# Row statistics of an encoder layer: column sums by a matrix of ones in split f32, root and Newton step on the whole tile

## The chip, the cores and the metric

The kernel runs on one core of one Trainium2 chip. The metric is the device time of one execution in microseconds; the time of a kernel is the median of its runs.

## The reference

One layer of a hybrid encoder in float32: 512 positions, 2048 channels.

```
x1  = rms_norm(x, g1);  proj = x1 @ w_in                       (5 x 1024 columns)
y_conv = silu(layer_norm(depthwise_conv31(u_val * sigmoid(u_gate))))
y_na   = neighbourhood attention of 16 heads on an 8 x 64 grid, with position bias
x  = x + concat(rms_norm(y_conv), rms_norm(y_na)) @ w_out
x2 = rms_norm(x, g2);  up = depthwise_conv3(x2 @ w_up)          (2 x 5632 columns)
x  = x + (silu(gate) * val) @ w_down
return rms_norm(x, g3)
rms_norm(x, g)   = x * rsqrt(mean(x*x) + 1e-6) * g
layer_norm(x)    = (x - mu) * rsqrt(var + 1e-6) * g + b
```

## The kernel before

The work lies transposed: channels on the 128 partitions, the 512 positions in the free dimension. A product is made by *split* matmuls: each f32 operand is written as a high part in the type f32r and the rest (`whi`, `wlo` for weights, lines 115 and 116; `xh`, `xl` and so on for data), and three f32r matmuls are added (`mm3`, lines 128, 131, 132). `weights()` keeps the splits of weights three units ahead of TensorE, in four buffers for each part; ScalarE makes the high part, VectorE the rest.

The order of stages: the input projection (`project`, one block of 512 positions by 128 columns after the other: 48 split matmuls each, results in three PSUM buffers of tag `mm`), with the convolution rows (`glu`, `gated`) and the attention of head pairs (`attend`) worked off behind it; the output projection in two halves (`out_half`: first the convolution group `ma`, then the attention group `mb`, 24 split matmuls for each of 16 blocks); the gated MLP with `w_up` (`up`, `hidden`) and `w_down`.

The normalisations are not applied to the operands but to results, as factors that are equal in all partitions: a tile of 128x512 that holds in each row the factor of each position. There are five of them:

- `rstd1` (from `acc1`): first used in `gated` (line 313) on the result of the first gate projection; with it all results of the input projection
- `rln` (from the `acc` of `group_a`): the LayerNorm of the convolution rows, after their mean (line 343)
- `ra`: used by `read_a` (line 532) on the results of the first half of the output projection
- `rna` (kept in `rb`): used by `after` on the results of the second half
- `rstd2`: used in `hidden` (lines 710 and 711) on the results of `up`

Squares are summed over channel tiles by `sum_sq` into an accumulator of 128x512; what remains is a sum over the 128 partitions, a root, and the factor in all partitions. `rsqrt_steps` does it in two steps. First: four f32 matmuls with a block of the accumulator as weights and one column of ones give the sums of 512 positions as 128x4 (line 216); mean and epsilon, `Sqrt`, reciprocal and one Newton step run on 128x4 (lines 219 to 225); four `tensor_scalar` scale the identity matrix into diagonals `dg` (line 229). Second: one f32 matmul of `dg` with ones spreads the factors over all partitions (line 232), and ScalarE copies them out (line 236).

The mean of the LayerNorm is made by one f32 matmul of the accumulator with ones (line 343).

Statistics are worked as generators: `tick` lets the next step of the first waiting generator be issued behind a block of matmuls. Apart from pinned instructions a scheduler of the framework puts the instructions of each engine in an order when the kernel is built; on the chip each engine works its queue in that order. SP issues the loads in its own order too: weights (`raw`, nine buffers, which the convolution rows `y` share) and the bias tables of the attention (`tab`).

`Sqrt`, `Sigmoid`, `Exp` and `Silu` belong to different function tables of ScalarE; a change of table is an instruction of its own in its queue.

Of the kernel before, what the change touches and what calls it, by code (L numbers as in the profile page):

```python
# [10 lines left out]
F32 = mybir.dt.float32  # L11
F32R = mybir.dt.float32r
AF = mybir.ActivationFunctionType
ALU = mybir.AluOpType
AX = mybir.AxisListType

P = 128
D = 2048
S = 512
# [9 lines left out]
EPS = 1e-6  # L29
# [41 lines left out]
def layer(ctx: ExitStack, tc: tile.TileContext, xT, w_in, w_out, w_up, w_down, par, tab, g3, out):  # L71
    nc = tc.nc
    consts = ctx.enter_context(tc.tile_pool(name="consts", bufs=1))
    wpool = ctx.enter_context(tc.tile_pool(name="w", bufs=3))
    tp = ctx.enter_context(tc.tile_pool(name="t", bufs=NT))
    sm = ctx.enter_context(tc.tile_pool(name="sm", bufs=2))
    dram = ctx.enter_context(tc.tile_pool(name="dram", bufs=1, space=bass.MemoryType.DRAM))
    psm = ctx.enter_context(tc.tile_pool(name="psm", bufs=3, space=bass.MemoryType.PSUM))
    psa = ctx.enter_context(tc.tile_pool(name="psa", bufs=1, space=bass.MemoryType.PSUM))
# [9 lines left out]
    def t2(name, dt=F32):  # L89
        return tp.tile([P, S], dt, tag="t2k", name=name)  # L90
# [8 lines left out]
    def pc(name, i):  # L99
        o = POFF[name] + i  # L100
        return prm[:, o:o + 1]

    ones = consts.tile([P, P], F32, name="ones")
    nc.vector.memset(ones, 1.0)
    ident = consts.tile([P, P], F32, name="ident")
    make_identity(nc, ident)

    def raw_unit(src, n):
        raw = t4([P, U * P], "raw")
        return raw, nc.sync.dma_start(raw[:, :n], src)  # L110
# [78 lines left out]
    def split(src, g, name):  # L189

        h, l = t2(name + "h", F32R), t2(name + "l", F32R)
        nc.scalar.activation(h, src, AF.Copy, scale=g)
        nc.vector.scalar_tensor_tensor(l, src, g, h.bitcast(F32), op0=ALU.mult, op1=ALU.subtract)
        return h, l

    def sum_sq(acc, src, first, to=slice(0, S)):
        if first:
            nc.scalar.activation(acc, src, AF.Square)
        else:
            q = t2("sq")[:, to]  # L200
            nc.scalar.activation(q, src, AF.Square)
            nc.vector.tensor_add(acc, acc, q)

    def stat():
        if where:
            return psa.tile([P, S], F32, tag="tr", name="st", bufs=2)
        return psa.tile([P, 2, S], F32, tag="sc", name="st")[:, 0]

    where = []

    def rsqrt_steps(acc, n, name, to=slice(0, S), keep=True):

        m = (to.stop - to.start) // P
        ps = stat()
        for i in range(m):
            nc.tensor.matmul(ps[:, i:i + 1], acc[:, to.start + i * P:to.start + (i + 1) * P], ones[:, 0:1],
                             start=True, stop=True)
        v, r, y = (sm.tile([P, S // P], F32, tag="rs" + c, name="rs" + c)[:, :m] for c in "vry")
        nc.vector.tensor_scalar(v, ps[:, :m], 1.0 / n, EPS, op0=ALU.mult, op1=ALU.add)
        nc.scalar.activation(r, v, AF.Sqrt)  # L220
        nc.vector.reciprocal(r, r)
        nc.vector.tensor_mul(y, v, r)
        nc.vector.tensor_mul(y, y, r)
        nc.vector.tensor_scalar(y, y, -0.5, 1.5, op0=ALU.mult, op1=ALU.add)
        nc.vector.tensor_mul(y, y, r)

        dg = t2("dg")
        for i in range(m):
            nc.vector.tensor_scalar(dg[:, i * P:(i + 1) * P], ident, y[:, i:i + 1], None, op0=ALU.mult)
        yield  # L230
        ps = stat()
        nc.tensor.matmul(ps[:, :m * P], ones, dg[:, :m * P], start=True, stop=True)
        if not keep:
            return ps[:, :m * P]
        res = t2(name)
        nc.scalar.activation(res[:, to], ps[:, :m * P], AF.Copy)
        return res

    def rsqrt_of(*a, **k):
        g = rsqrt_steps(*a, **k)  # L240
        while True:
            try:
                next(g)
            except StopIteration as e:
                return e.value


    xs, x1, early = [], [], []
# [3 lines left out]
    for k in range(KD):  # L252
        x1.append(t2("x"))
        last = pin(nc.sync.dma_start(x1[k], xT[k]))
        h, l = t2("xh", F32R), t2("xl", F32R)
# [3 lines left out]
        if k in (0, 2, 6, 15):  # L259
            raw, i = raw_unit(first[len(early)], U * P)  # L260
# [8 lines left out]
    for step in ORDER:  # L269
        i = next(a_ if step == "a" else q_)  # L270
# [9 lines left out]
    def stats1():  # L280
        for k in range(KD):
            sum_sq(acc1, x1[k], k == 0)
        for _ in range(3):
            yield
        rstd.append((yield from rsqrt_steps(acc1, D, "rstd1")))
# [48 lines left out]
    def group_a():  # L334
        yield
        yield
        acc = t2("acc")
        nc.vector.tensor_add(acc, ys[0], ys[1])
        for i in range(2, NC_):
            nc.vector.tensor_add(acc, acc, ys[i])  # L340
        yield
        ps = psa.tile([P, 2, S], F32, tag="sc", name="st")[:, 0]
        nc.tensor.matmul(ps, ones, acc, start=True, stop=True)
        mu = t2("mu")
        nc.vector.tensor_scalar(mu, ps, 1.0 / CONV, None, op0=ALU.mult)
        acc = t2("acc")
        for i in range(NC_):
            nc.vector.tensor_sub(ys[i], ys[i], mu)
            sum_sq(acc, ys[i], i == 0)
        yield  # L350
        yield
        r = yield from rsqrt_steps(acc, CONV, "rln")
        acc = t2("acc")
        for i in range(NC_):
            nc.vector.tensor_mul(ys[i], ys[i], r)
            nc.scalar.activation(ys[i], ys[i], AF.Silu, scale=pc("lng", i), bias=pc("lnb", i))
            ma.append(split(ys[i], pc("cog", i), "ma"))
        for i in range(NC_):
            sum_sq(acc, ys[i], i == 0)
        for _ in range(RA_AFTER):  # L360
            yield

        ra.append((yield from rsqrt_steps(acc, CONV, "ra")))
# [125 lines left out]
    p, n = -1, 0  # L489
    for step in ORDER:  # L490
        if step == "a":
            if n < 2:
                with tc.issue_after(last.ins):
                    glu(n)
            else:
                glu(n)
            n += 1
            continue
        p += 1
        steps.append(attend(p, *qkv(p)))  # L500
        if p == NORM_AT:
            asteps.append(group_a())
# [259 lines left out]
    def four(first):  # L762

        if first:
            b = psa.tile([P, 2, S], F32, tag="sc", name="pd2")
            return [b[:, 0], b[:, 1]] + [psa.tile([P, S], F32, tag="tr", name="pd", bufs=2) for _ in range(2)]
        return [psm.tile([P, S], F32, tag="mm", name="pd") for _ in range(3)] + [psa.tile([P, S], F32, tag="po",
                                                                                         name="pd")]
# [97 lines left out]
    a = four(True)  # L866
# [19 lines left out]
    a = four(True)  # L886
# [68 lines left out]
```

## Time and profile before

| | us |
|---|---|
| three runs, median (lowest to highest) | 2018.7 (2017.3 to 2019.84) |
| profiled execution | 2021.06 |
| its span | 2019.1 |
| granted TensorE clock, mean | 0.996 |

Times of rows in the profile count from the start of the span. A row of the timeline gives start, duration, engine, line, operation, output and inputs with their shape, and in brackets how long the engine was idle before it and what released it. A row of a group gives the count, the busy time, the mean duration in ns, and the idle time before it. `PE` is TensorE, `PEld` its loading of weights, `ACT` ScalarE, `DVE` VectorE, `SPq` the queue of loads. An f32 matmul counts as two records, an f32r matmul as one.

### The profile page before, as it was taken

How to read it: one execution, taken by the hardware profiler on the slowest of the kernel's cores; microseconds unless marked ns; L12 is line 12 of the kernel's file. 1: busy time of each engine (PE TensorE's matmuls, PEld its weight loads, DVE VectorE, ACT ScalarE, POOL GpSimd, SP SyncE). 2: the span in 40 equal slices, each digit the busy share in tenths (PEclk: the TensorE clock that was granted, in tenths of full speed). 3: DMA queues.
4: the chain of work that ended last, by engine and by line, in shares of the span. 5: the costliest groups of instructions: out<-in, count | busy, mean ns of one | idle time of the engine just before them, and what ended most of it. 6: DMA issues, size and time to landing. Idle time of an engine off the chain costs nothing.

```text
span 2019.1 us, 28450 instructions
## 1 busy us (share of the span) xinstructions
PE 1990.3 (99%) x10511; PEld 1682.7 (83%) x10511; DVE 1608.5 (80%) x2311; ACT 1104.1 (55%) x1724; POOL 230.2 (11%) x318
## 2 busy tenths in 40 slices
PE   8999999998999999999999999999999999999997
PEld 6888888877788888888888888888888888888886
DVE  7985798497556888888888888888888898886764
ACT  6244424446535666666666666666666654554663
POOL 0111111111001111111111111111110400000000
PEclk9999999999999999999999999999999999999999
DMA  7677677676758879899999898998986976665562
GB/s 257 167 222 182 171 176 207 175 191 196 232 140 214 209 204 253 248 247 256 249 255 258 245 267 233 264 242 256 259 236 192 344 261 217 213 217 192 194 212 101
DMA packets 141755, 446.81 MB, mean 221 GB/s; under 512 B 15920, under 2 KB 24112, under 8 KB 140208
## 3 DMA queue, kind: packets, MB, share of 16 engines
q1 hardware_dynamic: 98352, 293.99, 42.6%
q0 software_dynamic: 43264, 151.01, 34.4%
q8 instruction: 82, 1.34, 0.3%
q14 instruction: 57, 0.47, 0.1%
HBM read 426.07 MB, written 111.15 MB: 266 GB/s over the span
## 4 chain that ended last, share of the span: by engine, by line
PE 97%; ACT 1%; DMA 1%; DVE 1%; issue 0%; SPq 0%; POOLq 0%; POOL 0%; DVEq 0%
PE pu L656 25%; PE pu L659 12%; PE pj L128 7%; PE pj L132 7%; PE pd L778 7%; PE pd L779 7%; PE pd L777 7%; PE pj L131 7%; PE po L128 3%; PE po L131 3%; PE po L132 3%; PE pu L128 2%; PE pu L131 2%; PE pu L132 2%; PE po L454 1%; PE sc L414 1%
## 5 line engine op out<-in xcount | busy, mean ns | idle before, releaser
L115 ACT ACTIVATE whi<-raw 128x1024 fp32r<-128x1024 f32 x574 | 607.2, 1059 | 719.2 <-PE pj L131 220.6
L116 DVE TENSOR_TENSOR wlo<-raw,whi 128x1024 fp32r<-128x1024 f32 x574 | 701.1, 1222 | 295.5 <-ACT whi L115 268.2
L656 PE MATMUL pu<-xc,whi 128*128 128x512 f32 x2112 | 748.8, 399 | 0.0
L659 PE MATMUL pu<-xc,wlo 128*128 128x256 f32 x2112 | 593.2, 281 | 0.0
L656 PEld LDWEIGHTS pu<-xc,whi 128*128 128x128 f32 x2112 | 397.0, 188 | 97.0 <-issue 0.2
L659 PEld LDWEIGHTS pu<-xc,wlo 128*128 128x128 f32 x2112 | 399.1, 189 | 0.3 <-issue 0.2
L128 PE MATMUL pj<-xh,whi 128*128 128x512 f32 x640 | 254.4, 399 | 8.0 <-ACT whi L115 8.0
L131 PE MATMUL pj<-xl,whi 128*128 128x512 f32 x640 | 251.4, 393 | 0.0
L132 PE MATMUL pj<-xh,wlo 128*128 128x512 f32 x640 | 251.2, 393 | 0.0
L777 PE MATMUL pd<-whi,ho 128*128 128x512 f32 x616 | 239.5, 389 | 1.6 <-ACT ho L738 1.6
L779 PE MATMUL pd<-whi,ho 128*128 128x512 f32 x616 | 239.6, 389 | 0.6 <-DVE ho L739 0.6
L778 PE MATMUL pd<-wlo,ho 128*128 128x512 f32 x616 | 239.8, 389 | 0.0
L328 DVE SCALAR_TENSOR_TENSOR y<-ch,prm,y 128x507 f32<-128x507 f32 (+14 forms) x240 | 169.8, 739 | 3.3
L128 PEld LDWEIGHTS pj<-xh,whi 128*128 128x128 f32 x640 | 121.3, 189 | 36.3 <-ACT whi L115 9.4
L132 PEld LDWEIGHTS pj<-xh,wlo 128*128 128x128 f32 x640 | 120.9, 189 | 27.9 <-DVE wlo L116 1.5
L131 PEld LDWEIGHTS pj<-xl,whi 128*128 128x128 f32 x640 | 121.2, 189 | 24.7 <-issue 0.7
L184 POOL DMA_DIRECT2D ws<-in_w_down x88 | 79.4, 903 | 545.4 <-DMA ws<-ws 273.6
L777 PEld LDWEIGHTS pd<-whi,ho 128*128 128x128 f32 x616 | 115.7, 188 | 26.3 <-ACT ho L738 1.9
L779 PEld LDWEIGHTS pd<-whi,ho 128*128 128x128 f32 x616 | 115.7, 188 | 25.0 <-DVE ho L739 1.2
L778 PEld LDWEIGHTS pd<-wlo,ho 128*128 128x128 f32 x616 | 115.7, 188 | 24.1 <-DVE wlo L116 0.3
L605 POOL DMA_DIRECT2D raw<-in_w_up x88 | 85.3, 969 | 368.0 <-DMA raw<-in_w_up 142.2
L128 PE MATMUL pu<-xc,whi 128*128 128x256 f32 x352 | 99.7, 283 | 0.5 <-ACT xc L546 0.5
(170 smaller groups left out, 2500.4 us busy)
## 6 DMA issues: line engine op xcount, KB each, us to landing
raw<-in_w_up SPq DMA_DIRECT2D x220, 512.0 KB, 7.3
ws<-in_w_down POOLq DMA_DIRECT2D x132, 512.0 KB, 7.4
raw<-in_w_up POOLq DMA_DIRECT2D x88, 512.0 KB, 9.4
raw<-ws SPq DMA_DIRECT2D x88, 512.0 KB, 3.4
raw<-in_w_in SPq DMA_DIRECT2D x80, 512.0 KB, 5.0
raw<-in_w_down SPq DMA_DIRECT2D x66, 512.0 KB, 3.7
ws<-ws POOLq DMA_DIRECT2D x44, 512.0 KB, 7.2
raw<-in_w_out SPq DMA_DIRECT2D x32, 512.0 KB, 5.2
```

The lines of the kernel that those rows point to most:

```text
L115: i = nc.scalar.activation(hi[:, :n], raw[:, :n], AF.Copy)
L116: j = nc.vector.tensor_sub(lo[:, :n], raw[:, :n], hi[:, :n].bitcast(F32))
L128: i = nc.tensor.matmul(ps, hi[:, a], mh, start=start, stop=False, skip_group_check=more)
L131: nc.tensor.matmul(ps, hi[:, a], ml, start=False, stop=False, skip_group_check=more)
L132: return nc.tensor.matmul(ps, lo[:, a], mh, start=False, stop=stop, skip_group_check=more)
L328: nc.vector.scalar_tensor_tensor(y[:, a:b], h[:, a + j - PAD:b + j - PAD], prm[:, o + j:o + j + 1], y[:, a:b], op0=ALU.mult, op1=ALU.add)
L605: nc.gpsimd.dma_start(a[c], w_up[f, q2], accum_op=ALU.add)
L656: i = nc.tensor.matmul(ps, hi[:, w], m, start=k == 0 and not more, stop=False, skip_group_check=more)
L659: i = nc.tensor.matmul(ps[:, :H], lo[:, w], m[:, :H], start=False, stop=k == U - 1, skip_group_check=more)
L777: nc.tensor.matmul(ps[i], h[:, t], wh[:, d], start=start and not more, stop=False, skip_group_check=more)
L778: nc.tensor.matmul(ps[i], h[:, t], wl[:, d], start=False, stop=False, skip_group_check=more)
L779: return nc.tensor.matmul(ps[i], h[:, tl], wh[:, d], start=False, stop=stop, skip_group_check=more)
```

## The change

The sum over partitions is made in all partitions at once: the accumulator is split into a high part and a rest (`column_sum`), and two f32r matmuls with a matrix of ones as weights add them up into a PSUM tile of 128x512. Mean and epsilon, `Sqrt`, reciprocal and the Newton step then run on the whole tile of 128x512, one half on ScalarE (`Identity`, `Sqrt`, `Square`) and one half on VectorE. The diagonals, the second matmul and the copy are gone. The mean of the LayerNorm is made by `column_sum` too. The chain of one statistic is cut by a `yield` between the sum and the root. Lines of the changed kernel differ from those of the kernel before by +2 ahead of `column_sum` and by -10 or -11 behind `rsqrt_steps`.

```diff
-    ones = consts.tile([P, P], F32, name="ones")
-    nc.vector.memset(ones, 1.0)
+    ones_r = consts.tile([P, P], F32R, name="onesr")
+    nc.vector.memset(ones_r.bitcast(F32), 1.0)
+    eps = consts.tile([P, 1], F32, name="eps")
+    nc.vector.memset(eps, EPS)
...
-    def rsqrt_steps(acc, n, name, to=slice(0, S), keep=True):
-
-        m = (to.stop - to.start) // P
+    def column_sum(acc):
+
+        h, l = t2("ach", F32R), t2("acl", F32R)
+        nc.scalar.activation(h, acc, AF.Copy)
+        nc.vector.tensor_sub(l, acc, h.bitcast(F32))
         ps = stat()
-        for i in range(m):
-            nc.tensor.matmul(ps[:, i:i + 1], acc[:, to.start + i * P:to.start + (i + 1) * P], ones[:, 0:1],
-                             start=True, stop=True)
-        v, r, y = (sm.tile([P, S // P], F32, tag="rs" + c, name="rs" + c)[:, :m] for c in "vry")
-        nc.vector.tensor_scalar(v, ps[:, :m], 1.0 / n, EPS, op0=ALU.mult, op1=ALU.add)
-        nc.scalar.activation(r, v, AF.Sqrt)
+        nc.tensor.matmul(ps, ones_r, h, start=True, stop=False)
+        nc.tensor.matmul(ps, ones_r, l, start=False, stop=True)
+        return ps
+
+    def rsqrt_steps(acc, n, name):
+
+        ps = column_sum(acc)
+        yield
+        nc.scalar.activation(acc, ps, AF.Identity, scale=1.0 / n, bias=eps)
+        r, q = t2(name), t2("rq")
+        nc.scalar.activation(r, acc, AF.Sqrt)
         nc.vector.reciprocal(r, r)
-        nc.vector.tensor_mul(y, v, r)
-        nc.vector.tensor_mul(y, y, r)
-        nc.vector.tensor_scalar(y, y, -0.5, 1.5, op0=ALU.mult, op1=ALU.add)
-        nc.vector.tensor_mul(y, y, r)
-
-        dg = t2("dg")
-        for i in range(m):
-            nc.vector.tensor_scalar(dg[:, i * P:(i + 1) * P], ident, y[:, i:i + 1], None, op0=ALU.mult)
-        yield
-        ps = stat()
-        nc.tensor.matmul(ps[:, :m * P], ones, dg[:, :m * P], start=True, stop=True)
-        if not keep:
-            return ps[:, :m * P]
-        res = t2(name)
-        nc.scalar.activation(res[:, to], ps[:, :m * P], AF.Copy)
-        return res
...
+        nc.scalar.activation(q, r, AF.Square)
+        nc.vector.tensor_mul(q, q, acc)
+        nc.vector.tensor_scalar(q, q, -0.5, 1.5, op0=ALU.mult, op1=ALU.add)
+        nc.vector.tensor_mul(r, r, q)
+        return r
...
         yield
-        ps = psa.tile([P, 2, S], F32, tag="sc", name="st")[:, 0]
-        nc.tensor.matmul(ps, ones, acc, start=True, stop=True)
+        ps = column_sum(acc)
         mu = t2("mu")
```

More of the change, by code (lines that the diff above doesn't have):

```diff
@@ L209, in layer @@
     where = []
-    def rsqrt_steps(acc, n, name, to=slice(0, S), keep=True):
-        m = (to.stop - to.start) // P
+    def column_sum(acc):
+        h, l = t2("ach", F32R), t2("acl", F32R)
+        nc.scalar.activation(h, acc, AF.Copy)
+        nc.vector.tensor_sub(l, acc, h.bitcast(F32))
         ps = stat()
-        for i in range(m):
-            nc.tensor.matmul(ps[:, i:i + 1], acc[:, to.start + i * P:to.start + (i + 1) * P], ones[:, 0:1],
-                             start=True, stop=True)
-        v, r, y = (sm.tile([P, S // P], F32, tag="rs" + c, name="rs" + c)[:, :m] for c in "vry")
-        nc.vector.tensor_scalar(v, ps[:, :m], 1.0 / n, EPS, op0=ALU.mult, op1=ALU.add)
-        nc.scalar.activation(r, v, AF.Sqrt)
-        nc.vector.reciprocal(r, r)
-        nc.vector.tensor_mul(y, v, r)
-        nc.vector.tensor_mul(y, y, r)
-        nc.vector.tensor_scalar(y, y, -0.5, 1.5, op0=ALU.mult, op1=ALU.add)
-        nc.vector.tensor_mul(y, y, r)
-        dg = t2("dg")
-        for i in range(m):
-            nc.vector.tensor_scalar(dg[:, i * P:(i + 1) * P], ident, y[:, i:i + 1], None, op0=ALU.mult)
-        yield
-        ps = stat()
-        nc.tensor.matmul(ps[:, :m * P], ones, dg[:, :m * P], start=True, stop=True)
-        if not keep:
-            return ps[:, :m * P]
-        res = t2(name)
-        nc.scalar.activation(res[:, to], ps[:, :m * P], AF.Copy)
-        return res
[L239 to L245, printed above, removed]
+        nc.tensor.matmul(ps, ones_r, h, start=True, stop=False)
[7 more added lines that the diff above has]
+        nc.scalar.activation(r, acc, AF.Sqrt)
+        nc.vector.reciprocal(r, r)
+        nc.scalar.activation(q, r, AF.Square)
[3 more added lines that the diff above has]
+        return r
     xs, x1, early = [], [], []
```

## The prediction

> **What bounds the kernel now.** I read the page first (shares of the span, then the chain that ended last), then the timeline around each of the six places that the change touches, then the groups of instructions for durations, and the windows for the granted clock.
>
> ```profile
> PE 1990.3 (99%) x10511; PEld 1682.7 (83%) x10511; DVE 1608.5 (80%) x2311; ACT 1104.1 (55%) x1724; POOL 230.2 (11%) x318
> ...
> PE 97%; ACT 1%; DMA 1%; DVE 1%; issue 0%; SPq 0%; POOLq 0%; POOL 0%; DVEq 0%
> ```
>
> TensorE is the bound: 97% of the chain. A microsecond less of matmul is a microsecond less of time, unless TensorE then waits; and every new wait of TensorE is paid in full, since hardly any idle time is left to swallow it. So there are two questions: how much TensorE time the new sums save, and whether the new arithmetic on whole tiles makes TensorE wait.
>
> The first statistic shows both:
>
> ```profile
> 37.02 0.69 DVE L202 TENSOR_TENSOR acc<-acc,sq 128x512 f32<-128x512 f32 x1
> ...
> 37.62 1.22 DVE L116 TENSOR_TENSOR wlo<-raw,whi 128x1024 fp32r<-128x1024 f32 x1
> 37.67 0.39 PE L131 MATMUL pj<-xl,whi 128*128 128x512 f32 x1
> ...
> 39.03 0.39 PE L128 MATMUL pj<-xh,whi 128*128 128x512 f32 x1
> ...
> 41.75 0.40 PE L128 MATMUL pj<-xh,whi 128*128 128x512 f32 x1
> ...
> 43.04 0.60 ACT L236 ACTIVATE rstd<-st 128x512 f32<-128x512 f32 x1 [3.75 <-PE st L232]
> ...
> 43.31 0.40 PE L128 MATMUL pj<-xh,whi 128*128 128x512 f32 x1
> ...
> 43.67 0.69 DVE L313 TENSOR_TENSOR gate<-pj,rstd 128x512 f32<-128x512 f32 x1 [2.40 <-ACT rstd L236]
> ...
> 46.06 0.39 PE L128 MATMUL pj<-xh,whi 128*128 128x512 f32 x1
> ```
>
> From 39.03 to 41.75 lie twelve undisturbed split matmuls: 2.72/12 = 0.227 us each, the price of one f32r matmul of 512 columns. From 37.67 to 39.03 lie two of them (0.45) and the four column sums: these cost 1.36 - 0.45 = 0.91 us. From 41.75 to 43.31 lie three (0.68) and the f32 matmul on the diagonal: 1.56 - 0.68 = 0.88 us. The row at 46.06 begins the fourth projection. It is the first to take a PSUM buffer for a second time (three of tag mm) and so needs the gate product, which ends at 43.67 + 0.69 = 44.36. Spare time there: 1.7 us.
>
> **TensorE time saved.** Five roots lose 0.91 + 0.88 each, and the mean of the LayerNorm loses one f32 matmul like that on the diagonal (0.88): 9.8 us. Added are 6 x 2 = 12 f32r matmuls with the ones as weights, at 0.227: 2.7 us. Net **-7.1 us**.
>
> **The new chain behind each sum.** Prices by shape:
>
> ```profile
> L427 DVE RECIPROCAL su<-su 128x2 f32<-128x2 f32 x32 | 5.1, 162 | 14.5 <-ACT s L426 14.5
> L221 DVE RECIPROCAL rsr<-rsr 128x4 f32<-128x4 f32 x5 | 0.9, 177 | 5.5 <-ACT rsr L220 5.5
> L842 DVE RECIPROCAL rsr<-rsr 128x1 f32<-128x1 f32 x4 | 0.6, 158 | 0.3 <-ACT rsr L841 0.3
> L202 DVE TENSOR_TENSOR acc<-acc,sq 128x512 f32<-128x512 f32 x44 | 30.3, 689 | 6.8 <-ACT sq L201 4.9
> L324 DVE TENSOR_SCALAR y<-ch,prm 128x512 f32<-128x512 f32 x8 | 4.3, 540 | 0.0
> L201 ACT ACTIVATE sq<-x 128x512 f32<-128x512 f32 x30 | 17.5, 624 | 21.1 <-DVE x L565 21.1
> L573 ACT ACTIVATE b<-x,prm 128x512 f32<-128x512 f32 x16 | 10.6, 713 | 0.0
> L314 ACT ACT_TABLE_LOAD x4 | 5.1, 1283 | 0.1
> ```
>
> Ahead of the sum stand a copy (0.62) and a subtraction (0.69). Behind it: the Identity with a pointer bias 0.71 (as the pointer scale of L573), a table load 1.28 where another set was in use, Sqrt 0.62, the reciprocal, Square 0.62, a product 0.69, the tensor_scalar 0.54, a product 0.69. The reciprocal of 128x512 is nowhere in the trace. Its rows for 1, 2 and 4 columns (158, 162, 177 ns) lie on a line of 6.5 ns per element, which gives 0.158 + 511 x 0.0065 = **3.5 us**. The ends: 0.69, if it ran like the elementwise rows, and 0.162 + 510 x 0.0075 = 4.0 from the steepest pair. I take 3.5, since the three rows rise by 6.5 ns for each element, where the addition of 512 columns takes 689/512 = 1.3 ns for each. The Trainium skill (VectorE: DVE Perf Modes, First, the fixed hardware budget) says that the reciprocal is an iterative divide with a repeat count of 8; if that meant eight cycles for each element at 0.96 GHz it would be an estimated 4.4 us, and the sum below about 2 us larger.
>
> From Identity to the last product that is 8.65 us, and 0.3 for seven handovers between engines. The old small steps and their diagonal go, but on VectorE and ScalarE only; whether the chain costs time depends on who waits at its end.
>
> *First root (`rstd1`).* The sum's last addition ends at 37.71, the copy at 38.4; VectorE is in a weight split until 38.84 and subtracts until 39.55. In the changed build's queue of TensorE the first new matmul stands three split matmuls later than the old sums, the second five rows behind it: 38.58 and 39.71, both just in time. ScalarE sees the sum at 40.14. Its queue has the table load behind the Identity, which itself waits for the sum, so the load is not hidden any more. 40.14 + 8.65 + 0.3 = 49.1, and the gate product ends at 49.8. The fourth projection is due 22 rows behind the second new matmul, 39.71 + 22 x 0.227 = 44.7. TensorE waits **5.1 us**. With a reciprocal of 0.69 it would be 2.3, with 4.0 5.6.
>
> *`ra`.* The first half of the output projection holds its results in the same three buffers until `ra` is there:
>
> ```profile
> 530.26 0.39 PE L132 MATMUL po<-mah,wlo 128*128 128x512 f32 x1
> 532.05 0.66 PE L402 MATMUL trv<-ident,vw 128*128 128x128 f32 x4 [1.41 <-ACT pt L445]
> ...
> 534.08 0.47 PE L128 MATMUL po<-mah,whi 128*128 128x512 f32 x1
> ...
> 531.42 1.06 ACT L445 ACTIVATE pt<-trp 128x512 f32<-128x512 f32 x2
> 532.38 0.60 ACT L236 ACTIVATE ra<-st 128x512 f32<-128x512 f32 x1
> ...
> 533.01 0.69 DVE L532 TENSOR_TENSOR oa<-po,ra 128x512 f32<-128x512 f32 x1 [0.23 <-ACT ra L236]
> ```
>
> The third output block ends at 530.26; the fourth (534.08) needs the buffer that the product at 533.01 frees at 533.70. No spare time. ScalarE works in order, and its queue in the changed build reads: sum's Identity, two weight splits (the second waits for the end of the third block), the two `pt` copies, and only then the table load, Sqrt and Square. So the chain starts at 532.48 whatever the sum does: 1.28 + 0.62 + 3.5 + 0.62 + 0.69 + 0.54 + 0.69 + 0.3 = 8.2 later `ra` is there (540.7), and the product ends at 541.4 instead of 533.70. **+7.7 us** (4.9 to 8.2 with the ends of the reciprocal). Queued behind Square on ScalarE are `ao`, its split and the `vt` copies of the last head pair; they fit into the fourth block.
>
> *The clock.* A long wait has a second price (the last three numbers of a window's row are the granted clock, the DMA share and GB/s):
>
> ```profile
> 498.73 0.39 PE L131 MATMUL pj<-xl,whi 128*128 128x512 f32 x1
> 504.26 2.08 PE L414 MATMUL sc<-k,q 64*128 64x256 f32 x8 [5.14 <-DVE s L421]
> ...
> 498.00:504.00 6.00, 1.12 (x5) 0.58 (x4) 2.90 (x4) 0.45 (x2) 0.91 (x1) 0.87 1.03 419
> 504.00:509.00 5.00, 4.74 (x15) 3.32 (x16) 4.19 (x9) 3.33 (x12) 0.00 (x0) 0.50 1.00 272
> 509.00:515.00 6.00, 6.00 (x35) 5.21 (x34) 1.55 (x5) 4.71 (x13) 0.00 (x0) 0.98 0.07 12
> ```
>
> The one long wait of today's kernel (5.1 us) left a granted clock of 0.50 for the 5 us behind it, so 2.5 us were lost on top. The wait of 7.7 us gets the same: **+2.5**. The wait of 5.1 us lies at the edge of what one row can tell; I charge half: **+1.25**. By the Trainium skill (TensorE: Matmul & The Clock Gate, What's actually happening) the gate falls to half after an idle window of about 3.4 us, and the window runs freely; the trace agrees with one case (0.87 over 6 us puts the fall 1.6 us before 504). By that rule both waits are long enough to be hit, the shorter one only if the window lies well.
>
> *`rln` and the wait for the tables.* That long wait itself moves:
>
> ```profile
> 472.07 0.58 ACT L236 ACTIVATE rln<-st 128x512 f32<-128x512 f32 x1
> ...
> 489.01 1.10 SPq L464 DMA_DIRECT2D tab<-in_tab  x2
> ...
> 501.10 0.69 DVE L421 SCALAR_TENSOR_TENSOR s<-sc,tab 128x512 f32<-128x512 f32 x1 [5.96 <-DMA tab<-in_tab]
> ```
>
> The `tab` loads stand in SP's queue behind loads of `w_out`, into buffers that ScalarE's last passes over the convolution rows free. Those passes come about 7.5 us later (the chain of `rln` against the 0.58 copy), and one more such load stands ahead of the tables. Against that, the changed build puts the score matmuls 19 split matmuls later (4.3 us), and the two score additions follow each other without the weight split of 1.22 us between them. Tables issued at 496 with 8 to 12 us to land (12.1 today) let TensorE go on between 1.3 us later and 3 us earlier than now. I take **-1.0**, ends -5 (the wait falls short enough to keep the clock) and +2.
>
> *Mean, `rna` and `rstd2`.* At the mean and at `rstd2` the split of the sum has little cover; 0.4 us of wait each, **+0.8** (0 to 2.6, twice 0.62 + 0.69). `rna` is needed 32 us after it is made today, which covers everything. At `rstd2` no table load is needed, but the chain runs through VectorE while the accumulators are folded:
>
> ```profile
> 725.70 1.22 DVE L116 TENSOR_TENSOR wlo<-raw,whi 128x1024 fp32r<-128x1024 f32 x1 [1.80 <-ACT whi L115]
> ...
> 728.47 1.23 DVE L116 TENSOR_TENSOR wlo<-raw,whi 128x1024 fp32r<-128x1024 f32 x1 [1.22 <-ACT whi L115]
> 729.62 0.41 DVE L670 TENSOR_TENSOR vl<-vl,pu 128x256 f32<-128x256 f32 x1
> ...
> 732.98 1.06 ACT L115 ACTIVATE whi<-raw 128x1024 fp32r<-128x1024 f32 x1 [0.66 <-PE pu L656]
> ```
>
> The fold ends at 730.03; the next block of TensorE needs it at 733.0 (the weight split at 732.98 waits for the end of the product before). VectorE gets 0.69 + 3.5 + 1.92 more and 1.9 less to do ahead of it, 4.2 us, of which its idle 1.80 + 1.22 takes 3.0; TensorE comes 1.3 us earlier. 3.0 - 1.2 - 1.3 leaves 0.5 us of cover, less what the changed order costs: **+0.5** (0 to 1.5).
>
> **The sum.** -7.1 + 5.1 + 1.25 + 7.7 + 2.5 - 1.0 + 0.8 + 0.5 = +9.75. The profiled execution took 2021.06 us (span 2019.1 and 2.0 around it), so 2030.8 for one like it; it lies 2.4 above the median of the three runs, 2018.7, from which I forecast **2028.4 us**.
>
> **Rivals.** *TensorE time alone decides.* Its share of the chain speaks for it, and so would an earlier place of ScalarE's root in the queue: if `ra` were ready before the third output block ends and `rstd1` before 44.7, nothing would wait and the saving would stand: 2018.7 - 7.1 = 2011.6, faster. Against it speak the in-order queue at 532.38 and 1.7 us of spare time for an added 5. 8%. *A short reciprocal* (0.69): waits of 2.3 and 4.9, half a clock price (1.25), tables 3 us earlier: -7.1 + 2.3 + 4.9 + 1.25 - 3.0 + 0.8 = -0.9, 2017.8, no change. The three small reciprocals speak against it. 10%. *All at the dear ends* (reciprocal 4.0, clock price paid twice, tables late): -7.1 + 5.6 + 2.5 + 8.2 + 2.5 + 2.0 + 0.8 + 1.5 = +16.0, 2034.7. 20%. The forecast keeps 62%. That the change does not do what it says is excluded by the build: the new instructions are in the queues.
>
> **Numbers.** About 0.2% (4 us) is what a measurement of this kernel can tell from no change. Forecast and dear case are slower by more: 0.82; the short reciprocal is the same: 0.10; faster 0.08. The range 2019 to 2035 takes in the forecast and nearly all of the dear case, and leaves out the faster one and most of the short reciprocal.
>
> **What would show it.** Right: a row RECIPROCAL 128x512 near 3.5 us, five times; TensorE waiting some 5 us for a gate product near 45 us and some 7 us for `oa` at the fourth output block, with a granted clock of 0.50 behind it; matmuls of the sums at 0.23 us apart. Wrong: a reciprocal below 1 us, no wait of TensorE at the fourth projection, or the root of `ra` done while the third output block still runs.

## The result, and the profile after

| | before | after |
|---|---|---|
| median of runs, us | 2019.66 (6 runs, 2017.3 to 2029.33) | 2035.79 (6 runs, 2033.39 to 2040.69) |
| profiled execution, us | 2021.06 | 2034.95 |
| its span, us | 2019.1 | 2032.7 |
| granted TensorE clock, mean | 0.996 | 0.995 |

The changed kernel is slower: ratio 1.0079, 95% interval 1.0066 to 1.0091, 16.1 us between the medians and 13.6 us between the spans. The direction was forecast; the measured time lies 7.4 us above the forecast 2028.4 and 0.8 above the end of the range.

The page of the changed kernel, busy times and shares of the chain that ended last:

```profile
PE 1987.9 (98%) x10471; PEld 1679.9 (83%) x10471; DVE 1628.4 (80%) x2288; ACT 1112.3 (55%) x1735; POOL 231.0 (11%) x318
...
PE 72%; issue 20%; DVE 3%; ACT 3%; DMA 1%; POOL 0%; SPq 0%; POOLq 0%; ACTq 0%; DVEq 0%
```

TensorE works 2.4 us less than before, and VectorE and ScalarE now stand in the chain with 3% each. The 20% of "issue" are almost wholly two stretches behind 1628 us, where the chain runs along the POOL instructions of the output; TensorE is as busy there as before, and the stage table below shows no loss. The prices of the new operations, from the groups of instructions:

```profile
L230 DVE RECIPROCAL ra<-ra 128x512 f32<-128x512 f32 x1 | 3.4, 3353 | 1.7 <-ACT ra L229 1.7
L227 ACT ACTIVATE acc<-st,eps 128x512 f32<-128x512 f32 x4 | 2.7, 687 | 3.8 <-PE st L220 3.8
L233 DVE TENSOR_SCALAR rq<-rq 128x512 f32<-128x512 f32 x5 | 2.1, 424 | 0.1
```

The first root in the timeline of the changed kernel, and the clock behind it and behind `ra` in its windows:

```profile
41.83 0.69 ACT L227 ACTIVATE acc<-st,eps 128x512 f32<-128x512 f32 x1 [1.81 <-PE st L220]
42.54 1.28 ACT L229 ACT_TABLE_LOAD   x1
...
44.50 3.35 DVE L230 RECIPROCAL rstd<-rstd 128x512 f32<-128x512 f32 x1 [3.41 <-ACT rstd L229]
...
50.46 0.69 DVE L303 TENSOR_TENSOR gate<-pj,rstd 128x512 f32<-128x512 f32 x1
...
51.20 0.50 PE L130 MATMUL pj<-xh,whi 128*128 128x512 f32 x1 [4.64 <-DVE gate L303]
```

```profile
51.00:55.00 4.00, 3.80 (x10) 3.01 (x11) 3.23 (x6) 1.74 (x3) 0.00 (x0) 0.61 0.00 0
545.00:550.00 5.00, 4.93 (x12) 3.87 (x13) 4.56 (x8) 0.11 (x1) 0.00 (x0) 0.50 0.00 0
```

The reciprocal holds VectorE for 3.35 us, the fourth projection starts at 51.20, and a granted clock of 0.61 (0.50 behind `ra`) follows. `ra` in the same timeline:

```profile
535.32 1.07 ACT L434 ACTIVATE pt<-trp 128x512 f32<-128x512 f32 x2
536.41 1.28 ACT L229 ACT_TABLE_LOAD   x1
...
538.36 3.35 DVE L230 RECIPROCAL ra<-ra 128x512 f32<-128x512 f32 x1 [1.69 <-ACT ra L229]
...
544.33 0.69 DVE L521 TENSOR_TENSOR oa<-po,ra 128x512 f32<-128x512 f32 x1
...
545.07 0.80 PE L130 MATMUL po<-mah,whi 128*128 128x512 f32 x1 [6.73 <-DVE oa L521]
```

The root stands behind the two `pt` copies and TensorE waits 6.7 us for its end.

**Where the time goes, stage by stage.** I took the same matmul in TensorE's queue of two traces (for instance the 60th of the input projection with `xl,whi`) and the difference of its start against the profiled execution of the kernel before. What this difference gains within a stage is what the stage costs more. Stages by the time of the kernel before: first root 32 to 125 us, sums of mean and `rln` 125 to 497, tables and `ra` 497 to 541, `rna` 541 to 661, end of the output projection 661 to 710, `rstd2` 710 to 743, rest up to 1997. The rows from e_rstd1 on are the experiments of the next section.

| kernel | first root | mean, rln | tables, ra | rna | end of out | rstd2 | rest |
|---|---|---|---|---|---|---|---|
| forecast | +5.0 | -1.4 | +7.9 | -1.3 | 0 | -0.4 | 0 |
| after | +7.1 | -1.7 | +7.3 | -1.3 | +1.8 | -0.4 | 0.0 |
| e_rstd1 | +7.0 | 0.0 | -1.8 | -0.1 | +4.9 | +0.2 | -0.6 |
| e_ra | +1.0 | 0.0 | +6.4 | 0.0 | +0.7 | +0.3 | -0.6 |
| e_rest | +1.0 | -1.7 | +0.8 | -1.3 | +5.9 | +0.4 | +1.4 |
| e_rest2 | +0.4 | -1.7 | -0.1 | -1.3 | +5.3 | -0.3 | +1.3 |
| e_norecip | +2.0 | -1.7 | +0.2 | -1.3 | 0.0 | -0.4 | +1.4 |
| e_hoist | +6.6 | -1.8 | +7.6 | -1.3 | +0.1 | -0.6 | +1.6 |
| e_ra4 | +7.3 | -1.7 | +10.0 | -1.3 | -0.1 | -0.4 | 0.0 |
| e_ra4cut | +7.3 | -1.7 | +2.1 | -1.3 | +1.2 | -0.7 | 0.0 |
| e_ars | +0.6 | -1.8 | +3.9 | -1.3 | +1.8 | -0.4 | +1.3 |
| e_after_xt | +7.3 | -1.8 | +7.3 | -1.3 | -0.1 | -0.6 | +1.6 |
| e_before_xt | +0.9 | 0.0 | -2.4 | 0.0 | -0.1 | -0.3 | +1.5 |
| e_rest_xt | +1.2 | -1.7 | +1.0 | -1.3 | -0.1 | -0.6 | 0.0 |
| e_rest_ars | -0.1 | -1.7 | -1.9 | -1.3 | -0.1 | -0.9 | 0.0 |
| e_all_ars | +1.0 | -1.8 | -2.5 | -1.3 | -0.1 | -0.9 | +1.6 |

How far one trace can be trusted: at 32 us, before the first root, the traces lie between -1.2 and +1.7 us of the profiled execution of before. In the column of the first root the six other traces with the old root lie between -0.1 and +1.2, and nearly all of it arises from 32 to 36 us: four of them wait there 0.8 to 1.1 us for the split of a weight, as the changed kernel does (0.91 us at 35.33) and the profiled execution of before does not. From 36 to 125 us these six gain at most 0.05. The +1.3 to +1.6 of the last column is a halved clock: near 1590 us all sixteen traces have a wait of TensorE of 1.6 us and one of 0.6 us behind it, and in eight of them the granted clock fell there. The windows of e_norecip, and of before, where it did not fall:

```profile
1586.00:1590.00 4.00, 3.21 (x8) 2.30 (x9) 3.97 (x10) 2.36 (x7) 1.61 (x3) 0.65 1.03 398
```

```profile
1586.00:1590.00 4.00, 1.78 (x7) 1.14 (x7) 2.90 (x6) 3.04 (x8) 1.57 (x3) 1.00 1.03 400
```

### The profile page after: what moved, and what is told of

It reads as the page before. It is cut to its first block, busy times and chain, and to the rows that moved or that the text cites. A ratio compares the mean times of both kernels' runs of the same rounds, so it can differ in the third digit from the quotient of the medians.

```text
span 2032.7 us, 28340 instructions
## 1 busy us (share of the span) xinstructions
PE 1987.9 (98%) x10471; PEld 1679.9 (83%) x10471; DVE 1628.4 (80%) x2288; ACT 1112.3 (55%) x1735; POOL 231.0 (11%) x318
## 4 chain that ended last, share of the span: by engine, by line
PE 72%; issue 20%; DVE 3%; ACT 3%; DMA 1%; POOL 0%; SPq 0%; POOLq 0%; ACTq 0%; DVEq 0%
PE pu L645 24%; PE pu L648 12%; PE pj L130 6%; PE pj L134 6%; PE pj L133 6%; PE po L130 3%; PE po L133 3%; PE po L134 3%; PE pu L134 2%; PE pu L133 2%; PE pu L130 2%; DVE y L318 1%; ACT whi L117 1%; PE po L443 1%; PE sc L403 1%
```

## The experiments

The kernels were timed in four groups, each together with the kernel before; its medians were 2019.71 (23 runs), 2020.5 (17), 2019.63 (23) and 2020.04 (21). The last group (e_rest_ars and e_all_ars) ran on another chip than the other three, so its kernels are set against those of other groups by their ratios.

### One part at a time

Three kernels split the change: the whole tile for `rstd1` alone, for `ra` alone, and for the mean, `rln`, `rna` and `rstd2` together. The edit of the first (the function with the whole tile stands beside the old one):

```diff
-        rstd.append((yield from rsqrt_steps(acc1, D, "rstd1")))
+        rstd.append((yield from rsqrt_whole(acc1, D, "rstd1")))
```

> Against the kernel before, only rstd1 goes by the whole tile. Theory (waits where a result needs a buffer back): the two new matmuls save 0.91 + 0.88 - 2 x 0.227 = 1.3 us; TensorE waits about 4.8 us at the fourth projection for the gate product, the clock is halved behind it for some 3.4 us (1.9 us lost), and VectorE, held by the chain, is late at a weight split near 105 us (0.85 us): about +6 us, 2025 to 2027. Rival (TensorE time alone): -1.3 us. Rival (the larger loss lies in an interplay of the six places): less than half of +6. If the start (first weights) is again 1.7 us later than in the kernel before, the order of the loads or the constants makes it, not the statistic.

Measured 2028.32 us, ratio 1.0047 (1.0035 to 1.006): +8.6, above the 2025 to 2027 expected. Both rivals are refuted: the first root costs 7.0 by the stages, as in the changed kernel. The start is late again (first matmul by 1.3 us, 0.5 from the ninth `xl` matmul on), but e_norecip and e_ra4, with the same first instructions as the changed kernel, are 0.3 us early there: chance. On top come 4.9 us at the end of the output projection, a part of the code that this kernel does not touch, and 1.8 are given back at the tables.

```diff
-        ra.append((yield from rsqrt_steps(acc, CONV, "ra")))
+        ra.append((yield from rsqrt_whole(acc, CONV, "ra")))
```

> Against the kernel before, only ra goes by the whole tile. Theory: -1.3 us of TensorE time, a wait of 7.1 us for oa at the fourth output block and 2.4 us of halved clock behind it: about +8.2 us, 2026 to 2028. Rival (TensorE time alone): -1.3 us.

Measured 2028.76 us, ratio 1.0047 (1.0034 to 1.006): +9.0 where the theory had +8.2. TensorE's waits of this kernel from 495 to 560 us (total, times, longest):

```profile
PE po L131 <- DVE oa L551: 6.9, 1, 6.9
PE sc L433 <- DVE s L440: 3.8, 1, 3.8
```

```diff
+        ps = column_sum(acc)                    # the mean
...
-        r = yield from rsqrt_steps(acc, CONV, "rln")
+        r = yield from rsqrt_whole(acc, CONV, "rln")
...                                              # rna and rstd2 likewise
```

> Against the kernel before, the mean, rln, rna and rstd2 go by the new way, rstd1 and ra by the old one. Theory: 0.4 + 3 x 1.3 = 4.3 us of TensorE time saved, about 1 us more from the stage of the tables, 1 us lost at rstd2: about -4 us, 2014 to 2016, and so faster than both kernels. Rival (the longer chain costs VectorE or the loads elsewhere, the extra wait near 722 us among them): 0 or slower. If the wait of 1.75 us near 722 us is there again, it belongs to this part of the change and not to the shift in time that rstd1 and ra cause.

Measured 2020.53 us, ratio 1.0006 (0.9997 to 1.0014): no gain. The expectation of -4 failed. The three parts add up to 18.4 us, the whole change cost 16.1. In the trace of e_rest the 1.7 and 1.3 us of the sums are there, but +0.8 at the tables and +5.9 at the end of the output projection eat them. That end is the surprise; but this profiled execution took 2027.23 us and was the slowest of twelve, so that a loss of this size is not that of a typical run. There, ScalarE of this kernel waits:

```profile
706.74 0.72 ACT L564 ACTIVATE xc<-t 128x256 fp32r<-128x256 f32 x2 [4.88 <-DMA xt<-xt]
```

A tile `xc` takes a buffer of the common pool out of which `xt` is still being written to memory. The kernel before has no such wait.

> The run with mean, rln, rna and rstd2 alone once more, for its trace: in the first one TensorE stood 4.5 us near 706 us behind writes of xt to memory, with 1.4 us of halved clock. Theory (chance in the DMA's timing): the wait near 706 us is another one, between 0 and 4 us, and the time is 2018 to 2022. Rival (the change shifts that stage for good): again over 4 us and about 2027.

Measured 2024.81 us in its one run, and the wait again, one run of the same kernel later:

```profile
705.48 0.72 ACT L564 ACTIVATE xc<-t 128x256 fp32r<-128x256 f32 x2 [4.79 <-DMA xt<-xt]
```

So the wait is no accident of one execution. Its length varies between kernels (0.3 us in e_norecip, 0.5 in e_ra4, 1.2 in e_ra, 2.35 in the changed kernel, 4.0 in e_rstd1), and, as the median of e_rest suggests, between executions of one kernel; no trace of a run near that median was taken.

### What the buffers of xt cost

```diff
-        r = t2("xt").rearrange("p (t k) -> p t k", t=S // P)
+        r = tp.tile([P, S], F32, tag="xt", name="xt", bufs=3).rearrange("p (t k) -> p t k", t=S // P)
...
-NT = 75
+NT = 72
```

> The run with mean, rln, rna and rstd2 alone, with three buffers of their own for the tiles xt that are written out to memory (72 instead of 75 in the common pool). In all changed kernels a tile xc takes a buffer of the common pool out of which xt is still being written, ScalarE waits up to 4.9 us for that write and TensorE up to 4.5. Theory (the buffer is what costs): that wait is gone, the wait of TensorE near 706 us too, and 4 us come off: 2015 to 2018, below the kernel before. Rival (the writes are late whatever waits for them, and xt itself waits then): no change, 2020 to 2022.

> The changed kernel with three buffers of their own for xt. Theory: its wait of 1.75 us near 720 us goes: 1.5 to 2 us below the changed kernel, 2033.5 to 2034.5. Rival: no change.

> The kernel before with three buffers of their own for xt, as a control. It has no such wait: no change, 2018.5 to 2020.5. If it gains or loses over 2 us, the buffers do something else than to free xc.

Measured 2019.14 us (ratio 0.9995, 0.9986 to 1.0003), 2033.05 (1.0061, 1.0048 to 1.0074) and 2019.27 (0.9995, 0.9986 to 1.0003). In all three the column "end of out" falls to -0.1, and the wait of `xc` is gone. The changed kernel comes down by 2.7 us in the median, and by 1.9 in that stage of the traces; the control does not move. e_rest_xt came down by 1.4 only, less than expected, and stands beside the kernel before instead of 3 us below. So the collision of `xc` and `xt` is shown as one cost of the change, but it is not where the 4 us of TensorE time went.

### The tables and the chain of rln

What remains in e_rest_xt is the stage of the tables. VectorE before, with the sums of squares of the convolution rows and the `q` product:

```profile
487.94 5.46 DVE L202 TENSOR_TENSOR acc<-acc,sq 128x512 f32<-128x512 f32 x7
494.45 0.68 DVE L380 TENSOR_TENSOR q<-pj,rstd 128x512 f32<-128x512 f32 x1
```

The same in the changed kernel, and TensorE behind it:

```profile
507.19 0.69 DVE L204 TENSOR_TENSOR acc<-acc,sq 128x512 f32<-128x512 f32 x1 [0.47 <-DVE acc L204]
508.93 0.68 DVE L369 TENSOR_TENSOR q<-pj,rstd 128x512 f32<-128x512 f32 x1
509.76 0.76 PE L130 MATMUL po<-mah,whi 128*128 128x512 f32 x1 [2.95 <-DVE q L369]
```

`q` frees a PSUM buffer, and it stands behind sums that the chain of `rln` delays. It starts 14.5 us later, where TensorE is only 6.1 us later than before. The experiment shortens that chain:

```diff
-        nc.scalar.activation(r, acc, AF.Sqrt)
-        nc.vector.reciprocal(r, r)
+        nc.scalar.activation(r, acc, AF.Abs_reciprocal_sqrt)
         nc.scalar.activation(q, r, AF.Square)
```

> The run with mean, rln, rna and rstd2 alone and buffers of their own for xt, now with Abs_reciprocal_sqrt in place of Sqrt and the reciprocal in its three roots. Theory (the time saved ahead of the tables is eaten there because the chain of rln, 3.35 us longer by the reciprocal, brings the squares of the convolution rows later, and q, which frees a PSUM buffer, stands behind their sums on VectorE): the wait of 2.9 us for q falls to under 1, some of the halved clock goes, 2.5 to 4 us below the run with the reciprocal: 2015 to 2017, faster than the kernel before by about 0.15%. Rival (the landing of the bias tables sets that stage whatever rln does): within 1 us of 2019.

Measured 2016.1 us, ratio 0.9978 (0.997 to 0.9987): 3.9 us below the kernel before; e_rest_xt stood at 0.9995. TensorE's waits from 20 to 760 us, of e_rest_xt:

```profile
PE po L131 <- DVE q L398: 2.9, 1, 2.9
PE trp L459 <- ACT s L447: 2.2, 1, 2.2
```

and of e_rest_ars:

```profile
PE st L219 <- DVE s L438: 2.3, 1, 2.3
...
PE po L131 <- DVE q L397: 0.2, 1, 0.2
```

The wait for `q` is gone, and the stage goes from +1.0 to -1.9. The theory holds: the reciprocal with its handovers in the chain of `rln` cost 2.9 us at a place 25 us behind it. What is left there is the landing of the second tables (`s`, 2.3 us).

### The reciprocal and the table load

```diff
-        nc.vector.reciprocal(r, r)
+        nc.vector.tensor_scalar(r, r, 1.0, None, op0=ALU.mult)
```

> The changed kernel with the reciprocal of 128x512 replaced by a multiplication by 1 (the reciprocal is left out). Theory: the row of 3.35 us becomes about 0.43; the wait at the fourth projection falls from 4.8 to about 1.9 us and loses its halved clock and the late weight split (2.9 + 1.9 + 0.85), the wait for oa falls from 7.1 to 4.2 with up to 2.4 us of clock: 8 to 10 us below the changed kernel, 2026 to 2028. Rival (the waits are made by the place of the table load and the root in the queue of ScalarE, the reciprocal runs beside other work): less than 3 us below the changed kernel.

Measured 2022.11 us, ratio 1.0009 (1.0001 to 1.0018): 13.7 us below the changed kernel, more than the 8 to 10 expected. By the stages the first root gains 5.1 us, tables and `ra` together 7.1 (the wait for `q` shrinks from 2.95 to 0.73 us too), and 1.8 come from the end of the output projection. The late weight split stays (0.85 us again), against the expectation. TensorE's waits from 495 to 560 us:

```profile
PE po L130 <- DVE oa L521: 3.8, 1, 3.8
...
PE po L130 <- DVE q L369: 0.7, 1, 0.7
```

```diff
+    warm = consts.tile([P, 1], F32, name="warm")
+    nc.scalar.activation(warm, eps, AF.Sqrt)
```

> The changed kernel with one Sqrt of 128x1 at the start, so that the table for the first root is loaded while ScalarE waits for data. Theory: the load of 1.28 us leaves the chain of rstd1; the wait at the fourth projection falls from 4.8 to 3.5 us; if the clock falls only behind a wait of at least 3.4 us that also lies well, some or all of its 1.9 us go too: 1.3 to 3.2 us below the changed kernel, 2032.6 to 2034.5. Rival (the load is hidden anyway): no change.

Measured 2032.53 us, ratio 1.0054 (1.0036 to 1.0072): 3.3 us below the changed kernel. The wait at the fourth projection is 1.3 us shorter, and the clock falls all the same; timeline, then windows:

```profile
48.77 0.50 PE L132 MATMUL pj<-xh,whi 128*128 128x512 f32 x1 [3.35 <-DVE gate L305]
```

```profile
48.00:51.00 3.00, 2.23 (x6) 1.80 (x7) 2.25 (x4) 0.63 (x1) 0.00 (x0) 0.70 0.00 0
51.00:55.00 4.00, 4.00 (x15) 3.20 (x15) 3.89 (x7) 2.53 (x3) 0.00 (x0) 0.80 0.00 0
```

About 1.6 us are lost behind a wait of 3.35 us, as behind the 4.64 of the changed kernel; behind the 1.7 us of e_norecip the windows show 1.00. The column of the first root falls by 0.5 only, because this trace starts earlier (-1.2 against +0.7) and then waits 1.70 us for the split of a weight at 34.22, where the changed kernel waits 0.91. From 36 us on the root costs 4.9 us instead of 6.2: the early load is worth its 1.3 us. The rest of the 3.3 us lies elsewhere, above all at the end of the output projection (+0.1 against +1.8).

### The place of ra in the queues

```diff
-RA_AFTER = 5
+RA_AFTER = 4
```

> The changed kernel with RA_AFTER = 4 instead of 5: the sum for ra is offered one block of matmuls earlier, and in the queue of ScalarE the table load and the Sqrt then stand directly behind the sum's Identity, ahead of the two weight splits and the two pt copies. Theory (the price of ra lies in the place of the root in an in-order queue): Sqrt near 530 instead of 537.7, ra near 536, the wait for oa falls from 7.1 to under 1 us and its halved clock (2.4 us) goes: 8 to 10 us below the changed kernel, 2026 to 2028. Rival (the chain is simply too long, or VectorE held by the reciprocal delays a weight split by as much): less than 4 us below the changed kernel.

Measured 2036.24 us, ratio 1.0075 (1.0057 to 1.0093): no change, so the expectation failed. The wait for `oa` is gone, but another has taken its place. TensorE's waits up to 800 us, and VectorE's timeline:

```profile
PE po L130 <- DVE vw L378: 8.2, 1, 8.2
```

```profile
530.10 3.35 DVE L230 RECIPROCAL ra<-ra 128x512 f32<-128x512 f32 x1 [2.51 <-ACT ra L229]
...
535.04 0.42 DVE L378 TENSOR_TENSOR vw<-pj,rstd 128x256 f32<-128x256 f32 x1
```

The products `vw` also free a PSUM buffer. They now stand behind the reciprocal, for which VectorE waits 2.5 us with `vw` ready behind it; in the changed kernel `vw` ran at 526.45. The next run puts them ahead again:

```diff
+RA_AFTER = 4
...
         nc.scalar.activation(r, acc, AF.Sqrt)
+        if cut:                  # for ra alone
+            yield
         nc.vector.reciprocal(r, r)
```

> The changed kernel with RA_AFTER = 4 and, for ra alone, a yield between Sqrt and reciprocal. In VectorE's queue the four vw products (which free a PSUM buffer) then stand ahead of the reciprocal of ra again, where with RA_AFTER = 4 alone they stood behind it and cost 8.2 us; in ScalarE's queue Sqrt stands ahead of the weight splits, the Square still behind the pt copies. Theory (ra's price is the order of in-order queues): Square near 536.5, ra near 539, a wait for oa of about 2 us and no halved clock, none for vw: 7 to 8 us below the changed kernel, 2027 to 2029. Rival (every place of the chain costs the same, since some queue holds it): within 3 us of the changed kernel.

Measured 2029.2 us, ratio 1.0046 (1.0033 to 1.006): 6.6 us below the changed kernel, just short of the 7 to 8 expected. Of 6.7 us of wait 1.3 are left:

```profile
PE po L130 <- DVE oa L523: 1.3, 1, 1.3
```

The clock stays up behind it. By the starts of TensorE's matmuls from 529 to 541 us, the same operations on the same data cost 9.5 us at `ra` (6.7 of wait, most of the rest halved clock) or 1.7, by their place in two in-order queues. The whole stage gains only 5.2, since ahead of `ra` e_ra4cut loses 2.6 more than the changed kernel: it waits 2.07 instead of 1.66 us for `s`, and its clock falls behind that (0.57 from 521 to 525 us).

### Everything without the waits

```diff
+    nc.scalar.activation(warm, eps, AF.Abs_reciprocal_sqrt)     # at the start
...
-RA_AFTER = 5
+RA_AFTER = 4
...
-        nc.scalar.activation(r, acc, AF.Sqrt)
-        nc.vector.reciprocal(r, r)
+        nc.scalar.activation(r, acc, AF.Abs_reciprocal_sqrt)
```

> The changed kernel with Abs_reciprocal_sqrt on ScalarE in place of Sqrt and the reciprocal (the Newton step stays), its table loaded at the start as in the run with the early table load, and RA_AFTER = 4. Theory: with load and reciprocal gone from the chain of rstd1 (1.28 + 3.35 + two handovers) its wait of 4.8 us is nearly nothing and the clock stays up, ra comes in time, and the 7.1 us of TensorE time stand, less about 1 us for the order of VectorE's queue near 105 us and 0.5 us at the mean and rstd2: 2012 to 2015, faster than both kernels. Rival (other waits take the place of these): within 3 us of the kernel before.

Measured 2024.23 us, ratio 1.0018 (1.0005 to 1.0032). This is above the 2012 to 2015 expected and outside of the rival's 3 us, too. The first root is solved (+0.6), but this kernel has RA_AFTER = 4 without the cut, and pays what e_ra4 shows:

```profile
PE po L132 <- DVE vw L379: 5.0, 1, 5.0
```

The last kernel adds the three buffers of `xt` and, for `ra`, the cut:

```diff
+        if cut:                  # for ra alone
+            yield
+            nc.vector.tensor_mul(q, r, r)
+        else:
+            nc.scalar.activation(q, r, AF.Square)
```

> All six places by the new way, with every wait found so far taken away: Abs_reciprocal_sqrt for Sqrt and reciprocal, its table loaded at the start, RA_AFTER = 4 with a yield ahead of the Square of ra (which is made by VectorE there), three buffers of their own for xt. Theory: against the kernel before, 7.1 us of TensorE time saved, 2 us lost at the first root (0.3 of wait, 1.6 for the order of VectorE's queue near 105 us), 2 to 3 us gained at the tables, 1 us of wait for oa: 2011 to 2015. Rival (a queue holds the chain wherever it is put): 2018 or more.

Measured 2016.45 us, ratio 0.9982 (0.9973 to 0.9991): faster than the kernel before by 3.6 us, and 1.5 above the range expected. Its waits up to 760 us:

```profile
PE trp L435 <- ACT pt L439: 2.2, 1, 2.2
PE pj L136 <- DVE wlo L120: 1.9, 2, 1.4
PE po L132 <- DVE oa L526: 1.6, 1, 1.6
```

It and e_rest_ars are the two versions that beat both kernels; between them there is no difference that these runs can tell.

## Why the prediction was right and wrong

**TensorE time, right.** The sums of mean and `rln` gain 1.7 us in every trace that has them (0.43 + 1.33 worked out), `rna` 1.3. The 0.4 us of wait charged at the mean did not come.

**The reciprocal, right.** 3.35 us against 3.5: (3353 - 158)/511 = 6.25 ns per element, where the small rows gave 6.5. The Trainium skill's repeat count of 8 (VectorE: DVE Perf Modes, First, the fixed hardware budget), read as eight cycles for each element, gave an estimate of 4.4; the measurement decides against that reading.

**First root: 5.0 forecast, 7.1 measured, 6.2 of it behind 36 us.** The first 0.96 of the 7.1 lie ahead of the root, at the weight split of 35.33, where kernels with the old root wait as well. From 36 us on it is -1.3 for the sums, 4.8 of wait, 1.7 of clock and 0.95 at a weight split. The five traces with this root show 6.2 to 7.3 there; the halved clock lasts 3.41 us in the changed kernel and 6.83 in the other four. The wait was right (5.1, measured 4.64 on the row and 5.02 between two matmuls that else lie 0.23 apart). One term was mis-sized: the clock was charged half, 1.25; it cost 1.7, and it fell as well behind 3.35 us. The Trainium skill's window of about 3.4 us (TensorE: Matmul & The Clock Gate, What's actually happening) agrees with these lengths of 3.41 and twice 3.41 us. That the wait must fill such a window does not hold here: the clock fell behind the 2.95 us for `q` in the changed kernel, too:

```profile
509.00:513.00 4.00, 3.23 (x8) 2.64 (x9) 3.14 (x6) 0.00 (x0) 0.42 (x1) 0.57 1.03 395
```

One term was missing: the 0.95 us at a weight split. The timelines of VectorE before and after, then of TensorE after:

```profile
90.75 4.00 DVE L328 SCALAR_TENSOR_TENSOR y<-ch,prm,y 128x499 f32<-128x499 f32 x6
...
99.69 2.35 DVE L116 TENSOR_TENSOR wlo<-raw,whi 128x1024 fp32r<-128x1024 f32 x2
```

```profile
97.30 5.32 DVE L318 SCALAR_TENSOR_TENSOR y<-ch,prm,y 128x500 f32<-128x500 f32 x8
...
107.56 2.35 DVE L118 TENSOR_TENSOR wlo<-raw,whi 128x1024 fp32r<-128x1024 f32 x2
...
108.83 0.50 PE L134 MATMUL pj<-xh,wlo 128*128 128x512 f32 x1 [0.85 <-DVE wlo L118]
```

Eight convolution taps instead of six stand ahead of the split. The loss is 0.96 to 0.98 us with the reciprocal and without it (e_norecip), and 1.57 in e_ars, so it is not VectorE's load by the reciprocal; that the order which the scheduler gave makes it is argued from these rows, and no run changed that order alone.

**`ra`, right in mechanism, a little high.** 7.7 and 2.5 were charged. e_ra shows 6.9 of wait and, against the traces with both old roots in that stage (before 0, e_rstd1 -1.8, e_before_xt -2.4, mean -1.4), 7.8 for the stage, where -1.3 + 7.7 + 2.5 = 8.9 were forecast. The reason given, the root behind weight splits and `pt` copies in ScalarE's queue, is shown by e_ra4cut.

**`rln` and the tables: the term that failed.** I charged -1.0 with ends of -5 and +2, looking at when SP issues the tables. The issue was right: it came at 503.12, which is 496 and the 6.1 us by which TensorE was later, within 1 us. Missed was the `q` product: on VectorE it stands behind the same late squares, and TensorE waits for it. Against the profiled execution the pair hides this (the stages of after sum to +7.3 where +7.9 was forecast), because that execution waited 5.1 us for its tables; the other two traces with the old roots waited less, 2.5 in e_rstd1 (whose TensorE came later) and 3.4 in e_before_xt:

```profile
PE sc L414 <- DVE s L421: 3.4, 1, 3.4
```

Against the mean of those three (-1.4), the kernels with the new `rln` and the old `ra` (+0.8, -0.1 and +1.0) lose 2.0 at this stage: a term of +2, not -1. e_rest_ars shows the cause. In the changed kernel, tables and `ra` together lose 8.7 against that mean where 7.9 were forecast, since `ra` was charged too high.

**The end of the output projection: taken at nothing.** The prediction has no term for this stage. +1.8 in the profiled execution, gone with buffers of its own. Nothing in the changed lines touches it; that the four tiles of a root instead of two, all of the common pool, changed which buffer `xc` gets is the likely reason, and only the collision itself is shown.

**The base.** The median of before was 2018.7 in three runs and 2019.66 in six.

**Together.** Of the 7.4 us by which the forecast was short, 1.0 is the base. 2.2 lie between profiled executions and medians: that of before ran 1.4 us above its median of six, that of the changed kernel 0.8 below its own; 0.3 lie outside the spans. The spans differ by 13.6 where 9.75 was forecast. Of these 3.9, 1.7 arose ahead of 36 us (the start and the weight split there), which no run shows to be a cost of the change; the first root makes +1.2, the end of the output projection +1.8, the mean -0.4, and the tables with `ra` -0.5, as taken against an execution with a long wait for its tables. So three steps failed: the end of the output projection was left out, the first root had half a clock price and no late weight split, and the term of the tables missed the wait for `q`. The last one does not show in the sum, by luck.

The "dear ends" rival came near the measured time (2034.7) in part by luck: its late tables and a clock price paid twice came, its reciprocal of 4.0 us and its 1.5 us at `rstd2` did not, and the end of the output projection is not in it.

## What to carry to other kernels

Where an in-order engine sits between a result and the buffer that it frees, ask of each added operation what stands behind it in that queue and which of those free a buffer: at `ra` the same chain cost 9.5 or 1.7 us by its place, and moved without that question it only exchanged a wait for `oa` for one for `vw`. TensorE time saved ahead of a wait for something else (here the `q` product and the tables) is given back there; it pays only when the chain that ends the wait gets shorter too. And a single profiled execution is a base with its own luck: the trace of before showed a wait of 5.1 us for the tables, that of nearly the same kernel 3.4.

## What the runs showed of the hardware

- The reciprocal of 128x512 in f32 takes 3.353 us on VectorE, 6.25 ns per element, five times the 0.69 of an addition; `Abs_reciprocal_sqrt` on ScalarE followed by the same Newton step does without it.
- The `tensor_scalar` in f32 with two immediate operands from and to SBUF took 0.424 us for 128x512, less than the 0.54 with pointers that I had used.
- Behind each of the eighteen waits of TensorE of 3.35 to 8.2 us (20 us and later, sixteen traces) the granted clock fell to 0.50, at the latest 1.6 us behind its end, for 3.41 us or two or three times that; f32r matmuls of 512 columns then lie 0.43 us apart instead of 0.23. Within 2.5 us of the end of waits of 2.0 to 3.3 us it fell in thirteen of seventeen cases, behind the 1.7 us at the first root of e_norecip not, and behind the pair of 1.6 and 0.6 us near 1590 us in eight of sixteen traces.
